# Taking the high and the low part of an operand in one 512-column matmul, in four of seven up products and three of seven down products

## The chip, the cores and the metric

The kernel runs on one core of a Trainium2 chip. The metric is the device time of one execution in microseconds (us), less is better; the number for a kernel is the median of several executions. The profile is of one execution more, recorded by the hardware profiler.

Engines in the text: TensorE (PE in rows; PEld is its weight load), VectorE (DVE), ScalarE (ACT), GpSimd (POOL) and SyncE (SP). SP and POOL issue the transfers here.

## What is computed

One layer of a diffusion backbone over 512 tokens of width 2048 with 256 context tokens: modulated RMSNorm, an input projection, latent attention beside a gated short convolution, an output projection with a residual, and a gated MLP with a width-3 convolution over the tokens. All in float32. The change lies in the MLP:

```python
def conv_ffn(h, w_up, cw, cb, w_down):
    u = dwconv3(h @ w_up, cw, cb)
    a, g = jnp.split(u, 2, axis=-1)
    return (a * jax.nn.silu(g)) @ w_down
...
        hf_l = modulate(rms_norm(x, g_ffn_norm[l]), sh_f, sc_f)
        x = x + gt_f * conv_ffn(hf_l, w_up[l], ffn_conv_w[l], ffn_conv_b[l], w_down[l])
    return rms_norm(x, g_final)
```

`w_up` is 2048 x 11008 and `w_down` 5504 x 2048, so the MLP has 43 tiles of 128 hidden units, each with two up columns (gate and value).

## The kernel before

Activations are kept transposed: 128 features on the partitions, 512 tokens on the free axis. TensorE works on a short float format (float32r), so each float32 factor is split in a high part (a cast, on ScalarE) and a low part (the rest, a subtraction on VectorE). A product of a weight w and an operand x is three matmuls into one PSUM bank: w high by x high, w high by x low, w low by x high. That is `mm3` (L185 to L189, one line for each). Each matmul loads its own 128x128 weights first.

The MLP saves matmuls by Strassen's method in Winograd's form. Two feature tiles by two halves of the tokens (H0 and H1, 256 columns each) are a 2x2 block, and seven products of 256 columns stand in for eight. The operands are sums of such blocks, named "11", "21", "2", "1", "3", "4" and "22"; the products are p1, p2, p6, q5, p7, q4 and q3 in the order of those names.

*Up projection.* The first three of the 43 tiles are done plainly, row by row over 16 operand tiles (`row`, L612). The operand tiles `hf` have the high part in one buffer of 512 columns and the low part in another (`hf_tile`, L931), and so have the sums `TT` of `t_sums` (L1075). Then a loop (L1199) runs over the other 40 tiles f. Each has seven calls of `product` (L1165): `split4` (L995) splits 1024 columns of weights into one of three buffers (high by ScalarE, L998; low by VectorE, L999), and 8 times `mm3` follow, 24 matmuls of 256 columns. Three banks pa, pb and pc take p1, p6, p7 and q4 (pa), p2 (pb), q5 and q3 (pc). VectorE and ScalarE read them out into cg and ca (L1174, L1212, L1224, L1180, L1182); q4 and q3 of a tile are done a turn later, in `finish` (L1177). Then come the convolution and the gate (`acts`, L1010), and every second tile the sums for the down projection (`pair_sums`, L1035), whose results (tp) go to memory over POOL's queue with both parts side by side in 512 columns.

VectorE also adds weights: L1213 (a11 + s1, where s1 is a difference that an accumulating transfer on POOL's queue has made) and L1214.

*Down projection.* Seven hidden tiles are done plainly at 512 columns, the other 36 as 18 pairs: 24 steps (v0 to v23) of seven products over a window of 6 pairs, 18 matmuls each (`seven`, L1319). The operands come back from memory as tiles w with the parts side by side. `into` (L1331) adds a product into its sums in SBUF: L1335 in the first eight steps, L1338, with the gate as a factor, afterwards. Per step VectorE splits seven low parts (L999), makes s3 for the step after (L1290), and after POOL's accumulating transfer into s1 (L1291), which must come behind L1290, the sums L1351 and L1352. The last two steps, v22 and v23, run interleaved, and the final norm follows.

The order on each engine is not that of the code: the framework runs a model of the program over time and puts the instructions of each engine in the order in which they could go there. Each engine then works through its own list strictly, so an instruction that waits holds up all behind it.

Of the kernel before, what the change touches and what calls it, by code (L numbers as in the profile page):

```python
# [10 lines left out]
F32 = mybir.dt.float32  # L11
# [61 lines left out]
def block_kernel(ctx, tc, xt, ctxt, ctxn, c, c_ctx, w_ada, small, w_in, w_inc, w_q, w_kv, w_out,  # L73
# [111 lines left out]
    def mm3(ps, w, x, first, last, on_top=False):  # L185
        with tc.issue_after(behind.pop()) if behind else ExitStack():
            PE.matmul(ps, w[0], x[0], start=first, stop=False, skip_group_check=on_top)  # L187
        PE.matmul(ps, w[0], x[1], start=False, stop=False, skip_group_check=on_top)  # L188
        PE.matmul(ps, w[1], x[0], start=False, stop=last, skip_group_check=on_top)  # L189

# [734 lines left out]

    hf = {}

# [3 lines left out]
    def hf_tile(j, cols=slice(0, T)):  # L931
        if j not in hf:
            hf[j] = tuple(t2([P, T], F32R, f"hf{j}{z}") for z in "hl")
# [6 lines left out]
        hi, lo = (z[:, cols] for z in hf[j])  # L940
        A.copy(out=hi, in_=xr)
        ins = V.tensor_tensor(out=lo, in0=xr, in1=hi.bitcast(F32), op=ALU.subtract)
# [132 lines left out]
    def t_sums(j):  # L1075

        e, o = xres[2 * j], xres[2 * j + 1]
        i, c = j // 2, HS[j % 2]
        if j % 2 == 0:
            for n in (1, 2, 4):  # L1080
                TT[n, i] = tuple(t2([P, T], F32R, f"T{n}{i}{z}") for z in "hl")
# [11 lines left out]
        for n, src in ((1, e[:, H0]), (2, o[:, H1]), (4, o[:, H0])):  # L1093
            put(tuple(z[:, c] for z in TT[n, i]), src)

    def operand(n, j):
        if n in ("11", "3"):
            return half_of(hf[2 * j], n == "3")
        if n in ("21", "22"):
            return half_of(hf[2 * j + 1], n == "22")  # L1100
        return half_of(TT[int(n), j // 2], j % 2)
# [21 lines left out]

    pss = [bank_of(i, f"uf{g}") for g, i in enumerate((2, 3, 4, 5, 1, 0))]
# [3 lines left out]
    for k in range(EARLY):  # L1128
        row(pss, held[k], hf[k], k, H0)
        pump(1)  # L1130
    drain()
    for k in range(EARLY):
        hf_tile(k, H1)
        row(pss, held[k], hf[k], k, H1)
        pump(1)
        if k in (3, 5):
            t_sums(k // 2 - 1)
# [9 lines left out]
    for k in range(EARLY, NK):  # L1147
# [7 lines left out]
        row(pss, w, hf[k], k)  # L1155
# [8 lines left out]

    def product(ps, a, n, nm, first):  # L1165

        w = split4(a, 1024, nm)
        for j in range(8):
            mm3(ps[:, :256], part(w, j), operand(n, j), first and j == 0, j == 7, on_top=not first)
# [7 lines left out]
    def finish(st):  # L1177
        f, a22, s4, u2, u3, pa, pc, cg, ca = st
        product(pa, a22, "4", f"u{f}q4", False)
        A.activation(ca[:, H0], pa[:, :256], AF.Identity, scale=-1.0)  # L1180
        product(pc, s4, "22", f"u{f}q3", False)
        V.tensor_tensor(out=cg[:, H1], in0=pc[:, :256], in1=u2, op=ALU.add)  # L1182
        acts(f, cg, ca)
# [15 lines left out]
    for f in range(G // 2, NF):  # L1199
# [12 lines left out]
        V.tensor_tensor(out=cg[:, H0], in0=pb[:, :256], in1=u1, op=ALU.add)  # L1212
        V.tensor_tensor(out=a11, in0=a11, in1=s1, op=ALU.add)  # L1213
# [10 lines left out]
        V.scalar_tensor_tensor(out=ca[:, H1], in0=pc[:, :256], scalar=-1.0, in1=u3, op0=ALU.mult, op1=ALU.subtract)  # L1224
        if first_acts:
# [50 lines left out]
    def weights_of(st):  # L1276

        z = Step()
        z.st, z.win, z.m = st, window(st), 2 * (st % 8)
        nxt = window(st + 1) if st + 1 < STEPS else z.win  # L1280
# [38 lines left out]
    def seven(z, ps, a, n, nm, first, pump_at=()):  # L1319
# [3 lines left out]
        for j, p in enumerate(z.win):  # L1323
            x = win[n, p]
            mm3(ps[:, :256], part(w, j), (x[:, :256], x[:, 256:]), first and j == 0, j == WIN - 1, on_top=not first)
# [5 lines left out]
    def into(z, i, cols, ps, minus=False):  # L1331

        o = acc2[z.m + i][:, cols]
        if z.st < 8:
            ins = V.tensor_tensor(out=o, in0=o, in1=ps[:, :256], op=ALU.subtract if minus else ALU.add)  # L1335
        else:
            g = ng[:, z.m + i:z.m + i + 1] if minus else mod[:, 80 + z.m + i:81 + z.m + i]
            ins = V.scalar_tensor_tensor(out=o, in0=ps[:, :256], scalar=g, in1=o, op0=ALU.mult, op1=ALU.add)  # L1338
# [255 lines left out]
```

## Time and profile before

| | |
|---|---|
| median of 3 runs | 2148.93 us (2143.85 to 2150.8) |
| the profiled execution | 2158.83 us |
| its span, first to last instruction | 2157.0 us |
| mean granted TensorE clock | 0.994 |
| matmuls | 14458 |
| up projection by seven products | about 886 to 1695 us of the span |
| down projection by seven products | about 1770 to 2150 us |

The rows of a timeline have the start in us, the length in us, the engine, the line of the code, the operation and its tiles (out<-in, buffer numbers left out), the shapes, and in square brackets the idle time before it and what ended that. Matmuls are pipelined, so the next one starts before the recorded end of the last. A row of the stretches has the length, and for each engine its busy time and the number of instructions, then the granted clock of TensorE as a share, the mean busy share of the transfer engines and their GB/s. A row of waits has who waited, for whom, the total in us, the count and the longest.

### The profile page before, as it was taken

How to read it: one execution, taken by the hardware profiler on the slowest of the kernel's cores; microseconds unless marked ns; L12 is line 12 of the kernel's file. 1: busy time of each engine (PE TensorE's matmuls, PEld its weight loads, DVE VectorE, ACT ScalarE, POOL GpSimd, SP SyncE). 2: the span in 40 equal slices, each digit the busy share in tenths (PEclk: the TensorE clock that was granted, in tenths of full speed). 3: DMA queues.
4: the chain of work that ended last, by engine and by line, in shares of the span. 5: the costliest groups of instructions: out<-in, count | busy, mean ns of one | idle time of the engine just before them, and what ended most of it. 6: DMA issues, size and time to landing. Idle time of an engine off the chain costs nothing.

```text
span 2157.0 us, 37744 instructions
## 1 busy us (share of the span) xinstructions
PE 2104.9 (98%) x14458; PEld 1946.7 (90%) x14458; DVE 1769.0 (82%) x2859; ACT 1047.1 (49%) x1710; POOL 188.1 (9%) x270
## 2 busy tenths in 40 slices
PE   7899999999999999999999999999999999999997
PEld 4688788888888888999999999999999889999997
DVE  7998987778886889788888788788888658888877
ACT  5533333555552237555555555555555333333445
POOL 0000000000000000111211111111111000000000
PEclk9999999999999999999999999999999999999998
DMA  9979785334559986577887877877887999877683
GB/s 335 345 275 337 270 279 176 128 126 162 177 199 348 344 278 192 159 217 201 241 232 215 240 229 220 237 231 219 241 229 218 341 335 290 254 220 236 196 247 111
DMA packets 162121, 513.89 MB, mean 238 GB/s; under 512 B 18962, under 2 KB 23314, under 8 KB 156306
## 3 DMA queue, kind: packets, MB, share of 16 engines
q1 hardware_dynamic: 133364, 418.14, 56.5%
q0 software_dynamic: 27488, 92.29, 18.3%
q8 instruction: 113, 1.85, 0.3%
q10 hardware_dynamic: 1088, 1.05, 0.1%
q14 instruction: 68, 0.56, 0.1%
HBM read 464.22 MB, written 46.14 MB: 237 GB/s over the span
## 4 chain that ended last, share of the span: by engine, by line
PE 86%; DVE 6%; DMA 5%; issue 1%; ACT 1%; SPq 0%; DVEq 0%; POOLq 0%; ACTq 0%
PE pp L187 4%; PE pp L189 4%; PE pp L188 4%; PE o L189 1%; PE o L187 1%; PE o L188 1%; DMA ada<-in_w_ada 1%; PE d L187 1%; PE d L189 1%; PE d L188 1%; PE uf L187 1%; PE uf L188 1%; PE of L187 1%; PE of L188 1%; PE of L189 1%
## 5 line engine op out<-in xcount | busy, mean ns | idle before, releaser
L1044 POOL DMA_DIRECT2D t_d<-tp x126 | 71.9, 574 | 468.3 <-DVE tp L1043 465.4
L255 DVE SCALAR_TENSOR_TENSOR ada<-ada,sv 128x1024 f32<-128x1024 f32 x68 | 82.1, 1219 | 12.1 <-DMA ada<-in_w_ada 12.0
L166 ACT CAST w_0h<-rw 128x512 fp32r<-128x512 f32 (+1 forms) x63 | 38.3, 618 | 108.3 <-PE pp L188 63.1
L1121 POOL DMA_DIRECT2D u_s<-in_w_up x80 | 70.2, 878 | 224.4 <-DMA u_s<-in_w_up 131.5
L233 DVE SCALAR_TENSOR_TENSOR ada<-ada,sv 128x1024 f32<-128x1024 f32 x64 | 77.5, 1217 | 4.4 <-DMA ada<-in_w_ada 3.9
L522 DVE SCALAR_TENSOR_TENSOR ada<-ada,svc 128x1024 f32<-128x1024 f32 x64 | 76.0, 1220 | 2.3 <-DMA ada<-in_w_ada 2.3
L785 POOL TENSOR_TENSOR gr<-gr,half 128x8 f32<-128x8 f32 x4 | 10.1, 2524 | 628.7 <-DVE gr L784 536.8
L1042 ACT CAST tp<-a 128x256 fp32r<-128x256 f32 x90 | 34.7, 405 | 60.5 <-DMA t_d<-tp 54.1
L167 DVE TENSOR_TENSOR w_0l<-rw,w_0h 128x512 fp32r<-128x512 f32 (+1 forms) x63 | 42.6, 681 | 22.3 <-ACT w_0h L166 22.3
L255 DVE SCALAR_TENSOR_TENSOR ra<-ra,sv 128x1024 f32<-128x1024 f32 x44 | 52.5, 1217 | 1.1 <-DMA ra<-in_w_ada 1.1
L1213 DVE TENSOR_TENSOR u<-u,u_s 128x1024 f32<-128x1024 f32 x40 | 48.8, 1219 | 0.7 <-DMA u_s<-in_w_up 0.7
L1214 DVE TENSOR_TENSOR u<-u,u 128x1024 f32<-128x1024 f32 x40 | 48.7, 1218 | 0.0
L1043 DVE TENSOR_TENSOR tp<-a,tp 128x256 fp32r<-128x256 f32 x90 | 36.2, 418 | 12.3 <-ACT tp L1042 12.3
L756 ACT CAST pth<-t 128x384 fp32r<-128x384 f32 x64 | 28.6, 485 | 26.4 <-PE t L753 26.4
L1042 ACT CAST tp<-ts 128x256 fp32r<-128x256 f32 x36 | 14.6, 407 | 43.5 <-DMA t_d<-tp 41.1
L533 DVE TENSOR_TENSOR acc<-acc,pp 128x512 f32<-128x512 f32 x50 | 34.0, 680 | 2.1 <-PE pp L189 2.1
L757 DVE TENSOR_TENSOR ptl<-t,pth 128x384 fp32r<-128x384 f32 x64 | 33.2, 549 | 2.7 <-ACT pth L756 2.7
L737 DVE TENSOR_REDUCE mn<-s 128x1 f32<-128x768 f32 x32 | 30.4, 952 | 4.8 <-PE s L726 4.6
L1043 DVE TENSOR_TENSOR tp<-ts,tp 128x256 fp32r<-128x256 f32 x36 | 15.2, 421 | 23.3 <-ACT tp L1042 23.3
L1005 ACT ACTIVATE g<-cg,sm 128x512 f32<-128x512 f32 x40 | 32.5, 813 | 0.5 <-DVE cg L1182 0.5
L1005 ACT ACTIVATE a<-ca,sm 128x512 f32<-128x512 f32 x40 | 32.1, 803 | 0.0
L1013 ACT ACTIVATE g<-g 128x512 f32<-128x512 f32 x43 | 27.2, 632 | 6.4 <-DVE g L1007 6.4
(15967 smaller groups left out, 9398.2 us busy)
## 6 DMA issues: line engine op xcount, KB each, us to landing
ada<-in_w_ada SPq DMA_DIRECT2D x196, 512.0 KB, 6.0
u<-in_w_up SPq DMA_DIRECT2D x120, 512.0 KB, 8.2
w<-t_d SPq DMA_DIRECT2D x161, 256.0 KB, 5.2
u_s<-in_w_up SPq DMA_DIRECT2D x80, 512.0 KB, 4.3
u_s<-in_w_up POOLq DMA_DIRECT2D x80, 512.0 KB, 8.9
t_d<-tp POOLq DMA_DIRECT2D x126, 256.0 KB, 4.9
v<-in_w_dnw SPq DMA_DIRECT2D x72, 384.0 KB, 5.4
ra<-in_w_ada SPq DMA_DIRECT2D x22, 1024.0 KB, 4.9
```

What stands on the lines that cost most here:

```text
L187: PE.matmul(ps, w[0], x[0], start=first, stop=False, skip_group_check=on_top)
L188: PE.matmul(ps, w[0], x[1], start=False, stop=False, skip_group_check=on_top)
L189: PE.matmul(ps, w[1], x[0], start=False, stop=last, skip_group_check=on_top)
L233: V.scalar_tensor_tensor(out=r, in0=r, scalar=1.0, in1=vec[:, i * 1024:(i + 1) * 1024], op0=ALU.mult, op1=ALU.mult, accum_out=col[:, i:i + 1])
L255: keep(V.scalar_tensor_tensor(out=r, in0=r, scalar=1.0, in1=svs[i], op0=ALU.mult, op1=ALU.mult, accum_out=lc[:, t % 4:t % 4 + 1] if i else ...
L522: keep(V.scalar_tensor_tensor(out=raw[q], in0=raw[q], scalar=1.0, in1=svc[:, q * 1024:(q + 1) * 1024], op0=ALU.mult, op1=ALU.mult, accum_o ...
L1005: A.activation(u, src, AF.Identity, bias=s("fb", m), scale=s("fw", 86 + m))
L1042: A.copy(out=z[:, :256], in_=src)
L1043: V.tensor_tensor(out=z[:, 256:], in0=src, in1=z[:, :256].bitcast(F32), op=ALU.subtract)
L1044: G_.dma_start(t_d[p, OPS.index(n)], z.bitcast(F32))
L1121: G_.dma_start(r[-1], src[more], accum_op=ALU.add)
L1213: V.tensor_tensor(out=a11, in0=a11, in1=s1, op=ALU.add)
```

## The change

A new helper `mm2` takes an operand of 512 columns, the high part in the lower 256 and the low part in the upper. One matmul with the high weights runs over all 512 columns, and one with the low weights over the lower 256. The bank then holds w high by x low in its upper half, and VectorE adds that half to the destination in an operation of its own. In the up projection this holds for p2, q5, q4 and q3 (operands "21", "1", "4" and "22") of all 40 tiles; in the down projection for p2, q5 and q3 of the steps v0 to v21. The others keep `mm3`.

For that the operands must lie side by side: the odd tiles of `hf` become two tiles of 512 columns, one for each half of the tokens, and so do all `TT`. The plain rows over odd `hf` tiles run in two halves of 256 columns for that reason (`up_row`).

```diff
+    def mm2(ps, w, x, first, last, on_top=False):
+        n = x.shape[1] // 2
+        with tc.issue_after(behind.pop()) if behind else ExitStack():
+            PE.matmul(ps[:, :2 * n], w[0], x, start=first, stop=False, skip_group_check=on_top)
+        PE.matmul(ps[:, :n], w[1], x[:, :n], start=False, stop=last, skip_group_check=on_top)
...
+    def side_by_side(z, src):
+        n = T // 2
+        A.copy(out=z[:, :n], in_=src)
+        return V.tensor_tensor(out=z[:, n:], in0=src, in1=z[:, :n].bitcast(F32), op=ALU.subtract)
...
+        else:
+            for h in range(2):
+                if cols in (HS[h], slice(0, T)):
+                    hf[j, h] = t2([P, T], F32R, f"hf{j}{h}")
+                    ins = side_by_side(hf[j, h], xres[j][:, HS[h]])
...
+    def up_row(w, k, hs=(0, 1)):
+        if k % 2 == 0:
+            row(pss, w, hf[k], k, slice(hs[0] * 256, hs[-1] * 256 + 256))
+            return
+        for g in range(G):
+            for h in hs:
+                mm3(pss[g][:, HS[h]], w[g], two(hf[k, h]), False, k == NK - 1 and h == 1)
...
+    APART = ("21", "1", "4", "22")
+    def beside(dst, ps, minus=False):
+        V.tensor_tensor(out=dst, in0=dst, in1=ps[:, 256:], op=ALU.subtract if minus else ALU.add)
...
-            mm3(ps[:, :256], part(w, j), operand(n, j), first and j == 0, j == 7, on_top=not first)
+            x = operand(n, j)
+            if n in APART:
+                mm2(ps, part(w, j), x, first and j == 0, j == 7, on_top=not first)
+            else:
+                mm3(ps[:, :256], part(w, j), x if isinstance(x, tuple) else two(x), first and j == 0, j == 7, on_top=not first)
...
         A.activation(ca[:, H0], pa[:, :256], AF.Identity, scale=-1.0)
+        beside(ca[:, H0], pa, True)
         product(pc, s4, "22", f"u{f}q3", False)
         V.tensor_tensor(out=cg[:, H1], in0=pc[:, :256], in1=u2, op=ALU.add)
+        beside(cg[:, H1], pc)
...
         V.tensor_tensor(out=cg[:, H0], in0=pb[:, :256], in1=u1, op=ALU.add)
+        beside(cg[:, H0], pb)
...
         V.scalar_tensor_tensor(out=ca[:, H1], in0=pc[:, :256], scalar=-1.0, in1=u3, op0=ALU.mult, op1=ALU.subtract)
+        beside(ca[:, H1], pc, True)
...
+        z.apart = st < STEPS - 2
...
+            if z.apart and n in APART[:2] + APART[3:]:
+                mm2(ps, part(w, j), win[n, p], first and j == 0, j == WIN - 1, on_top=not first)
+            else:
+                mm3(ps[:, :256], part(w, j), two(win[n, p]), first and j == 0, j == WIN - 1, on_top=not first)
...
+        for x in (ps[:, :256], ps[:, 256:])[:2 if z.apart and ps is not z.pa else 1]:
+            if z.st < 8:
+                ins = V.tensor_tensor(out=o, in0=o, in1=x, op=ALU.subtract if minus else ALU.add)
+            else:
+                g = ng[:, z.m + i:z.m + i + 1] if minus else mod[:, 80 + z.m + i:81 + z.m + i]
+                ins = V.scalar_tensor_tensor(out=o, in0=x, scalar=g, in1=o, op0=ALU.mult, op1=ALU.add)
```

Three places show what moves. The lines of the changed kernel have numbers of their own: 1024 there is 999 before, 1257 and 1258 are 1213 and 1214, 1337 is 1290, 1388 is 1338, 1401 and 1402 are 1351 and 1352. The new addition in the up projection is 1200.

TensorE at the start of product p2 of up tile 20 (bank u20b; hf are operand tiles, u20p2h and u20p2l the two parts of the weights), before:

```order
L187 MATMUL u20b<-hf1h,u20p2h 128x256
L188 MATMUL u20b<-hf1l,u20p2h 128x256
L189 MATMUL u20b<-hf1h,u20p2l 128x256
L187 MATMUL u20b<-hf3h,u20p2h 128x256
L188 MATMUL u20b<-hf3l,u20p2h 128x256
L189 MATMUL u20b<-hf3h,u20p2l 128x256
```

and after the change:

```order
L196 MATMUL u20b<-hf_7575,u20p2h 128x512
L197 MATMUL u20b<-hf_7575,u20p2l 128x256
L196 MATMUL u20b<-hf_7676,u20p2h 128x512
L197 MATMUL u20b<-hf_7676,u20p2l 128x256
L196 MATMUL u20b<-hf_7691,u20p2h 128x512
L197 MATMUL u20b<-hf_7691,u20p2l 128x256
```

Three instructions per operand tile have become two, with the same number of columns in all.

VectorE from the low part of p1 of up tile 21 on, around that of p2 (u21p2l; the sum of u_11 and u_s is the one that waits for the accumulating transfer; a, g, ts and tp belong to the convolution and the sums for the down projection), before:

```order
L1213 TENSOR_TENSOR u_11_12589<-u_11_12589,u_s_12593 128x1024
L1015 TENSOR_TENSOR a_12748<-a_12748,g_12743 128x512
L999 TENSOR_TENSOR u21p2l<-u_12_12591,u21p2h 128x1024
L1048 TENSOR_TENSOR ts_13016<-a_12748 128x256
L999 TENSOR_TENSOR u20q4l<-u_22_12349,u20q4h 128x1024
L1214 TENSOR_TENSOR u_12_12591<-u_12_12591,u_11_12589 128x1024
```

and after:

```order
L1086 SCALAR_TENSOR_TENSOR a_12125<-ts_12158,a_12125 128x256
L1040 TENSOR_TENSOR a_12365<-a_12365,g_12360 128x512
L1024 TENSOR_TENSOR u21p2l<-u_12_12229,u21p2h 128x1024
L1257 TENSOR_TENSOR u_11_12227<-u_11_12227,u_s_12231 128x1024
L1068 TENSOR_TENSOR tp_12354<-a_12125,tp_12354 128x256
L1073 TENSOR_TENSOR ts_12605<-a_12365 128x256
L1024 TENSOR_TENSOR u20q4l<-u_22_12015,u20q4h 128x1024
```

The sum of u_11 has gone from ahead of u21p2l to behind it.

VectorE in the down projection, from the low part of p1 of step 13 on (c are the sums; v13b and v11c the banks of p2 and of q5 and q3; v13s and v14s the weights that the accumulating transfers change), before:

```order
L999 TENSOR_TENSOR v13p1l<-v_21392,v13p1h 128x768
L1351 TENSOR_TENSOR v_21392<-v_21392,v13s_21393 128x768
L1338 SCALAR_TENSOR_TENSOR c_18809<-v11c,mod,c_18809 128x256
L999 TENSOR_TENSOR v13p2l<-v_21394,v13p2h 128x768
L1338 SCALAR_TENSOR_TENSOR c_19122<-v12a,gn,c_19122 128x256
L1352 TENSOR_TENSOR v_21394<-v_21394,v_21392 128x768
L999 TENSOR_TENSOR v12q4l<-v_21199,v12q4h 128x768
L1338 SCALAR_TENSOR_TENSOR c_19124<-v13a,mod,c_19124 128x256
L999 TENSOR_TENSOR v13p6l<-v_21392,v13p6h 128x768
L1290 TENSOR_TENSOR v14s_21592<-v_21589,v14s_21590 128x768
L1338 SCALAR_TENSOR_TENSOR c_19124<-v13b,mod,c_19124 128x256
```

and after:

```order
L1388 SCALAR_TENSOR_TENSOR c_17789<-v11c,mod,c_17789 128x256
L1401 TENSOR_TENSOR v_20197<-v_20197,v13s_20198 128x768
L1388 SCALAR_TENSOR_TENSOR c_17789<-v11c,mod,c_17789 128x256
L1024 TENSOR_TENSOR v13p2l<-v_20199,v13p2h 128x768
L1388 SCALAR_TENSOR_TENSOR c_18102<-v12a,gn,c_18102 128x256
L1024 TENSOR_TENSOR v12q4l<-v_20019,v12q4h 128x768
L1402 TENSOR_TENSOR v_20199<-v_20199,v_20197 128x768
L1388 SCALAR_TENSOR_TENSOR c_18104<-v13a,mod,c_18104 128x256
L1024 TENSOR_TENSOR v13p6l<-v_20197,v13p6h 128x768
L1388 SCALAR_TENSOR_TENSOR c_18104<-v13b,mod,c_18104 128x256
L1337 TENSOR_TENSOR v14s_20382<-v_20379,v14s_20380 128x768
L1388 SCALAR_TENSOR_TENSOR c_18104<-v13b,mod,c_18104 128x256
```

The additions out of v11c and v13b come twice, one of each pair on either side of a sum; the first one out of v13b is now ahead of the sum of v14s; and the low part of q4 is ahead of the sum of v_20199 and no longer behind it.

36 lines of the change are left out of this document (15 added, 21 removed).

## The prediction

> **What bounds the kernel now.** I read the page first, then the busy time by stretch, then the timelines of TensorE and VectorE inside the two stages that the diff touches, then who waits for whom.
>
> The head of the page gives the span and each engine's share:
>
> ```profile
> span 2157.0 us, 37744 instructions
> PE 2104.9 (98%) x14458; PEld 1946.7 (90%) x14458; DVE 1769.0 (82%) x2859; ACT 1047.1 (49%) x1710; POOL 188.1 (9%) x270
> ```
>
> TensorE is busy 98% of the span and VectorE 82%. A busy share says little about pipelined matmuls, so I went on to stretches. The rows are the up projection, the first down steps, the middle ones and the tail:
>
> ```profile
> core 0: us, PE busy (x) PEld busy (x) DVE busy (x) ACT busy (x) POOL busy (x), PEclk, DMA share, GB/s
> 895.00:1695.00 800.00, 798.99 (x6647) 798.23 (x6646) 656.33 (x867) 454.99 (x681) 140.16 (x209) 1.00 0.80 229
> 1775.00:1850.00 75.00, 74.34 (x620) 73.59 (x619) 65.15 (x110) 28.80 (x35) 3.74 (x5) 1.00 0.92 292
> 1850.00:2060.00 210.00, 210.00 (x1753) 210.00 (x1752) 174.76 (x248) 83.37 (x101) 11.58 (x14) 1.00 0.76 225
> 2060.00:2157.00 97.00, 80.69 (x646) 78.48 (x644) 71.37 (x110) 47.99 (x85) 3.41 (x4) 0.94 0.56 169
> ```
>
> In the up projection TensorE has no gap (798.99 of 800 us) at a granted clock of 1.00; VectorE is at 82%. The middle down steps are the same (210 of 210 us, VectorE 83%). What one matmul costs is the distance between starts, not its recorded length. Here are the ends of one product of the up projection (tile 19, product p2), 24 matmuls of 256 columns, and the first of the next one:
>
> ```profile
> 1204.14 0.28 PE L187 MATMUL u19b<-hf1h,u19p2h 128*128 128x256 f32 x1
> ...
> 1207.02 0.28 PE L187 MATMUL u18a<-T40h,u18q4h 128*128 128x256 f32 x1
> ```
>
> 24 starts in 2.88 us: 120.0 ns each. The output projection has the same work 512 columns wide, 44 matmuls from the first row to the second:
>
> ```profile
> 739.70 0.39 PE L187 MATMUL o<-mx13h,o9w1536h 128*128 128x512 f32 x1
> ...
> 749.92 0.39 PE L189 MATMUL o<-mx11h,o10w1024l 128*128 128x512 f32 x1
> ```
>
> 10.22 us / 44 = 232.3 ns. So 512 columns in one matmul cost 7.7 ns less than in two (240.0). That is all that the change can win on TensorE, many times over.
>
> **The change, part by part.**
>
> *The matmuls.* In the up projection 40 tiles x 4 products x 8 triples = 1280 triples of 256 columns become a pair of 512 and 256; in the down projection 22 steps x 3 products x 6 = 396. A triple costs 3 x 120.0 = 360.0 ns. For the pair, alternating widths are hardly in the trace; the nearest rows are the attention scores, five matmuls of 512 columns and then five of 256:
>
> ```profile
> 505.25 0.40 PE L722 MATMUL s<-kl11h,q11h 128*128 128x512 f32 x1
> ...
> 506.41 0.28 PE L722 MATMUL s<-kcx,q11h 128*128 128x256 f32 x1
> ...
> 507.00 0.69 PE L371 MATMUL qr<-xq,kc 128*128 128x512 f32 x1
> ```
>
> From 505.25 to 507.00 five of each take 1.75 us: 350 ns per pair, with no penalty where the width changes. The two paces above give 232.3 + 120.0 = 352.3. I take 351: 9 ns per triple (bounds 7.7 and 10). Up: 1280 x 9 = 11.5 us (9.9 to 12.8). Down: 396 x 9 = 3.6 us (3.0 to 4.0). All of it lies on TensorE, which has no gap there, so it is on the path as long as nobody else makes TensorE wait.
>
> The Trainium skill, "TensorE: Matmul & The Clock Gate", Back-to-back issue gap, gives N / 2.4 + 2.5 ns for a warm matmul: an estimate from that page is 109.2 ns at 256 columns and 215.8 at 512, so a triple would save only 2.6 ns and the whole change 4.4 us. The trace disagrees with both numbers (120.0 and 232.3 at a granted clock of 1.00).
>
> *The first product by rows.* Odd operand tiles now lie as two half tiles, so from tile 6 on the rows of 7, 9, 11, 13 and 15 run as 36 matmuls of 256 columns and not 18 of 512: 90 pairs x 7.7 ns = 0.7 us more. Splitting such a tile in two halves adds an operation each on ScalarE and VectorE, beside a row of 18 x 232.3 ns = 4.2 us on TensorE; nothing without that cover, 0.4 us a tile at the most.
>
> *VectorE's additions, up.* Each product that takes both parts leaves its second half in the upper 256 columns, and VectorE must add it: four more operations per tile. The nearest row reads a bank and adds, in the finishing of a tile:
>
> ```profile
> 1234.88 0.42 DVE L1182 TENSOR_TENSOR cg<-u19c,u 128x256 f32<-128x256 f32 x1
> 1235.22 0.41 DVE L1061 SCALAR_TENSOR_TENSOR a<-ts,a 128x256 f32<-128x256 f32 x1
> ```
>
> The next one starts 0.34 us later: 4 x 0.34 = 1.4 us per tile, 0.42 each where one must wait for the other's result. A tile takes 7 x 24 x 120 ns = 20.16 us, of which VectorE is idle 18%, 3.6 us. It has 2.2 us left, less the 0.3 us by which the tile gets shorter. So VectorE stays under TensorE on the mean; what counts is the queue in front of the low parts of the weights. The tightest one in the up projection is p2 of the odd tiles:
>
> ```profile
> 1242.84 1.22 DVE L999 TENSOR_TENSOR u21p2l<-u,u21p2h 128x1024 fp32r<-128x1024 f32 x1
> ```
>
> ```profile
> 1244.70 0.28 PE L189 MATMUL u21b<-hf1h,u21p2l 128*128 128x256 f32 x1
> ```
>
> The low part is done at 1244.06 and read at 1244.70: 0.64 us to spare, the least in steady state. In the new order the big sum of this tile goes behind u21p2l and not in front of it, which gives back 1.1 us of the 1.4. I take 1.0 us of new waits for the whole stage; bounds are zero and 20 odd tiles x 0.4 us = 8 us.
>
> *VectorE's additions, down.* Three more per step, in the middle steps of the form of L1338. Here VectorE also feeds itself: its sum for the next step (L1290) must be done before the accumulating transfer that POOL issues, and the step after next to it begins with L1351, which waits for that transfer. The rows are one turn of that loop, the low part q4 in it, and the transfer:
>
> ```profile
> 1977.00 0.96 DVE L1351 TENSOR_TENSOR v<-v,v14s 128x768 f32<-128x768 f32 x1 [1.02 <-DMA v14s<-in_w_dnw]
> 1980.40 0.95 DVE L999 TENSOR_TENSOR v13q4l<-v,v13q4h 128x768 fp32r<-128x768 f32 x1
> 1981.27 0.48 DVE L1338 SCALAR_TENSOR_TENSOR c<-v14a,mod,c 128x256 f32<-128x256 f32 x1
> 1981.66 0.95 DVE L999 TENSOR_TENSOR v14p6l<-v,v14p6h 128x768 fp32r<-128x768 f32 x1
> 1982.65 0.96 DVE L1290 TENSOR_TENSOR v15s<-v,v15s 128x768 f32<-128x768 f32 x1
> ```
>
> ```profile
> L1291 POOL DMA_DIRECT2D v15s<-in_w_dnw x1: 850/850/850, 1984.1 to 1984.1; - x1
> ...
> DMA to landing us min/median/max: 5.1/6.8/7.8
> ```
>
> From L1351 to POOL's issue it is 7.1 us, the transfer takes 6.8 (5.1 to 7.8): 13.9 us of the step's 126 x 120 ns = 15.12. An addition costs 0.39 us (1981.27 to 1981.66). In the new order one of the three stands between L1351's successor and L1290's, since the one after p2 now comes ahead of the sum: 14.3 us of the new step's 14.96 (15.12 less 18 x 9 ns), 15.3 where the transfer takes 7.8. The low part of q4 goes ahead of the second big sum, 0.87 us earlier, so it loses nothing. Some steps wait already; of TensorE's waits in the down projection:
>
> ```profile
> PE v19a L189 <- DVE v19q4l L999: 0.9, 1, 0.9
> PE v20a L189 <- DVE v20q4l L999: 0.9, 1, 0.9
> PE v21a L189 <- DVE v21q4l L999: 0.9, 1, 0.9
> ```
>
> Such steps, some seven at both ends of the stage, turn with the loop and not with TensorE, and each becomes longer by the addition in it: 7 x 0.39 = 2.7 us. The bounds are zero and all three additions uncovered in every step, 22 x 3 x 0.42 = 28 us; I take the loop's 2.7, since the middle steps have room.
>
> *The sum.* -11.5 + 0.7 + 1.0 - 3.6 + 2.7 = -10.7 us. The profiled execution took 2158.83 us (span 2157.0, 1.8 around it) and would take 2148.1. The runs' median is 2148.93, 9.9 us below the profiled one; the same difference gives 2138.
>
> **The rivals.**
>
> *A: the remaining 256-column matmuls get faster as well.* The pace of 120.0 ns holds through the whole up projection, but in the first down steps it is less:
>
> ```profile
> 1775.51 0.28 PE L188 MATMUL v0a<-w,v0p6h 128*128 128x256 f32 x1
> ...
> 1780.49 0.28 PE L188 MATMUL v0a<-w,v0p7h 128*128 128x256 f32 x1
> ```
>
> 42 starts in 4.98 us are 118.6 ns. So 120.0 is not what 256 columns need; a stream of mixed widths could leave that beat. Then 3 x 24 x 1.4 ns x 40 = 4.0 us come on top, the pair costs 350, and with few waits it is -12.8 - 4.0 - 4.0 + 0.7 = -20 us: 2129. Against it: the up projection comes out of a row product 512 columns wide and is at 120.0 at once.
>
> *B: the beat holds for the wide ones too.* If starts between 256-column matmuls keep to multiples of 120 ns, the pair takes 240 + 120 = 360 and nothing is won; the same result on the clock if waits for VectorE eat the 11 us. For it: the exact 120.0. Against it: the scores change from 512 to 256 without loss. TensorE then takes as long as now, so few waits are new; with the 0.7 of the rows it is 2150, within the bound of no change. The page's rule above stands close to it: less the same cost its 4.4 us would give an estimate of 2145.
>
> *C: VectorE becomes the bound, and it is slower.* The loop of L1351, L1290 and the transfer has 0.6 us left with a transfer of 6.8. It decides from the point where the transfer takes over 7.4 us on the mean. From step 18 to 19 the loop already took 16.1 us, with an addition of squares in it:
>
> ```profile
> 2036.54 0.96 DVE L1351 TENSOR_TENSOR v<-v,v18s 128x768 f32<-128x768 f32 x1
> ...
> 2052.64 0.96 DVE L1351 TENSOR_TENSOR v<-v,v19s 128x768 f32<-128x768 f32 x1 [1.06 <-DMA v19s<-in_w_dnw]
> ```
>
> At 16.1 us a step, 16 steps from 6 to 21 lose 16 x 1.0 = 16 us; with 8 us of waits at the odd tiles of the up projection and 11.5 won, it is +13: 2162. Against it: the transfer's median of 6.8, and a new order that was made with the additions in it.
>
> **How the numbers follow.** A measurement of this kernel tells about 0.3% (6.4 us) from no change. Forecast 0.57, A 0.15, B 0.18, C 0.10. The time is the forecast's, 2138. Low is A with a little more, 2127; high is B, 2150; beyond it lie C and the worse half of B. The forecast crosses 6.4 us where waits reach 5.5 us more than I took: 3 in 57 of it count as no change. Faster 0.54 + 0.15 = 0.69, same 0.03 + 0.18 = 0.21, slower 0.10.
>
> **What would show it.** Right: one product of the four in the up projection takes 8 x 351 = 2.81 us and not 2.88, a tile 19.88 us with 7 products, no wait of TensorE over 0.5 us in it, VectorE at 90%. Wrong in size: the pair at 360 (B), or p1, p6 and p7 under 2.86 us (A). Wrong in kind: TensorE waiting for low parts in the steps 6 to 18, or L1351's successor waiting for its transfer over 2 us in each (C).

## The result: slower by 3.2%, 2218.17 us

The changed kernel takes 2218.17 us in the median of 4 runs (2215.94 to 2222.97), the kernel before 2149.86 in the median of 4 (2143.85 to 2155.02). The ratio is 1.0322, with a 95% interval of 1.029 to 1.0354. The forecast was 2138, and none of the rivals came to this time.

The head of the page of the changed kernel, and the busy time of its up projection and of its middle down steps (columns as in the prediction: the stretch and its length, PE, PEld, DVE, ACT, POOL, granted clock, DMA share, GB/s):

```profile
span 2216.3 us, 34748 instructions
...
PE 2112.3 (95%) x12872; PEld 1878.4 (85%) x12872; DVE 1845.8 (83%) x3090; ACT 1051.9 (47%) x1715; POOL 187.7 (8%) x270
```

```profile
895.00:1695.00 800.00, 755.86 (x5027) 699.93 (x5025) 668.90 (x962) 431.22 (x638) 132.49 (x197) 0.97 0.75 211
...
1920.00:2110.00 190.00, 186.81 (x1347) 176.14 (x1348) 169.16 (x262) 73.52 (x90) 11.08 (x13) 1.00 0.74 219
```

TensorE, which had no gap in the up projection before (798.99 of 800 us), now stands still for 44 of 800 us, and the granted clock is 0.97 and no longer 1.00. VectorE is hardly busier in this stretch than before (84% against 82%), although it has four operations more per tile, because fewer tiles fall into these 800 us.

Where the 59.3 us between the two spans arise is read from the first matmul of each stage:

| stage (TensorE) | before | after | difference |
|---|---|---|---|
| all ahead of the first product by rows | 815.16 | 810.42 | -4.7 |
| first product by rows | 69.3 | 71.0 | +1.7 |
| up projection, seven products a tile | 801.8 | 856.7 | +54.9 |
| down projection, plain steps | 83.9 | 87.9 | +4.0 |
| down projection, seven products a step, to the last matmul | 376.8 | 380.2 | +3.4 |

The first line is no effect of the change: in the runs below this part ends anywhere from 810.0 to 817.3 us. Nor is the fourth: of its 4.0 us, 2.1 are one wait for a load in this execution, and a run below with the same order takes 84.1 us there.

**The matmuls did what was forecast.** In TensorE's timeline, product q5 of tile 18 with the wide matmuls, and p6 with the narrow ones:

```profile
1200.20 0.28 PE L187 MATMUL u18a<-T,u18p6h 128*128 128x256 f32 x1
...
1202.34 0.28 PE L187 MATMUL u18a<-T,u18p6h 128*128 128x256 f32 x1
...
1202.69 0.40 PE L196 MATMUL u18c<-T,u18q5h 128*128 128x512 f32 x1
...
1205.15 0.40 PE L196 MATMUL u18c<-T,u18q5h 128*128 128x512 f32 x1
```

From the third row to the fourth are seven pairs: 2.46 us, 351 ns each. From the first to the second are six triples: 2.14 us, 357 ns each, so the narrow ones run at 118.9 ns and not at 120.0 (rival A's pace). A tile without a wait takes 19.77 us; it took 20.16.

**The loss is at p1 of the odd tiles.** TensorE's waits in the up projection, longest first (who waits, on whom; us in total, times, longest):

```profile
PE u13a L187 <- ACT u13p1h L1023: 4.2, 1, 4.2
PE u25a L187 <- ACT u25p1h L1023: 3.8, 1, 3.8
...
PE u37a L187 <- ACT u37p1h L1023: 2.2, 1, 2.2
```

There are 15 of them, from tile 13 to 41, every second tile, 43.6 us in all. Nothing of the kind was there before. They wait for ScalarE's high part of the weights, not for VectorE's low part. ScalarE's timeline at tile 19, after and then before (L1067 and L1042 are the cast of a pair sum into its tile tp; in brackets the idle time ahead of an instruction and who ended it):

```profile
1202.10 0.81 ACT L1030 ACTIVATE a<-ca,sm 128x512 f32<-128x512 f32 x1
1206.92 0.40 ACT L1067 CAST tp<-a 128x256 fp32r<-128x256 f32 x1 [4.02 <-DMA t_d<-tp]
1207.23 1.04 ACT L1023 CAST u19p1h<-u 128x1024 fp32r<-128x1024 f32 x1
1208.18 0.37 ACT L1215 COPY u<-u18a 128x256 f32<-128x256 f32 x1
```

```profile
1195.58 1.05 ACT L998 CAST u19p1h<-u 128x1024 fp32r<-128x1024 f32 x1 [0.41 <-PE u18a L188]
1196.54 0.36 ACT L1174 COPY u<-u18a 128x256 f32<-128x256 f32 x1
1199.68 0.41 ACT L1042 CAST tp<-a 128x256 fp32r<-128x256 f32 x1 [2.78 <-DMA t_d<-tp]
```

Before, the cast into tp waited 2.78 us with the p1 weights already cast. After, it waits 4.02 us, and the p1 weights of tile 19 and the copy of bank u18a stand behind it. It waits for its buffer: only two t2 buffers rotate among the pair sums, and a buffer is free when its store has landed. The store it waits for, in POOL's timeline, and its way to landing (KB, us) in the list of transfers:

```profile
1196.01 0.86 POOL L1144 DMA_DIRECT2D u_s<-in_w_up  x1 [1.01 <-DMA u_s<-in_w_up]
1196.58 0.86 POOL L1069 DMA_DIRECT2D t_d<-tp  x1
```

```profile
t_d<-tp POOLq DMA_DIRECT2D x1, 256.0 KB, 10.3
```

Issued at 1196.58, it lands 10.3 us later, at 1206.9: that is when the cast starts. The median store lands after 5.2 us; this one was issued right behind an accumulating load of 512 KB. TensorE at the same place:

```profile
1205.38 0.28 PE L197 MATMUL u18c<-T,u18q5l 128*128 128x256 f32 x1
1208.33 0.39 PE L187 MATMUL u19a<-hf0h,u19p1h 128*128 128x256 f32 x1 [2.66 <-ACT u19p1h L1023]
...
1208.67 0.31 PE L187 MATMUL u18a<-hf0h,u18p7h 128*128 128x256 f32 x1
...
1209.12 0.41 PE L187 MATMUL u18a<-hf2h,u18p7h 128*128 128x256 f32 x1
...
1212.11 0.40 PE L189 MATMUL u18a<-hf10h,u18p7l 128*128 128x256 f32 x1
```

Two matmuls of p1 stand ahead of p7 of the tile before (in the kernel before as well), so TensorE stops as soon as q5 is through. When it goes on, 14 starts take 2.99 us, 213.6 ns each instead of 119: half clock, about 1.5 us more (the granted clock from 1208.90 to 1212.30 is 0.51, behind it 1.00). Counted in starts, the 14 long gaps up to tile 39 come to 42.3 us and the half clock behind them to 19.2 us: 61.5 us.

### The profile page after: what moved, and what is told of

It is laid out like the page before. It is cut to its first block, busy times and chain, and to the rows that moved or that the text cites. A ratio compares the mean times of both kernels' runs of the same rounds, so it can differ in the third digit from the quotient of the medians.

```text
span 2216.3 us, 34748 instructions
## 1 busy us (share of the span) xinstructions
PE 2112.3 (95%) x12872; PEld 1878.4 (85%) x12872; DVE 1845.8 (83%) x3090; ACT 1051.9 (47%) x1715; POOL 187.7 (8%) x270
## 4 chain that ended last, share of the span: by engine, by line
PE 66%; DMA 16%; DVE 11%; issue 3%; ACT 3%; POOL 0%; DVEq 0%; SPq 0%; POOLq 0%; ACTq 0%
DMA t_d<-tp 7%; DMA u_s<-in_w_up 4%; PE pp L187 4%; PE pp L189 4%; PE pp L188 4%; PE o L188 1%; PE o L187 1%; PE o L189 1%; DMA ada<-in_w_ada 1%; PE d L187 1%; PE uf L187 1%; PE uf L188 1%; PE uf L189 1%; PE d L188 1%; PE of L188 1%
## 5 line engine op out<-in xcount | busy, mean ns | idle before, releaser
L1069 POOL DMA_DIRECT2D t_d<-tp x126 | 78.9, 626 | 525.0 <-DVE tp L1068 513.7
L1144 POOL DMA_DIRECT2D u_s<-in_w_up x80 | 69.8, 872 | 233.9 <-DMA u_s<-in_w_up 147.3
L1067 ACT CAST tp<-a 128x256 fp32r<-128x256 f32 x90 | 34.8, 406 | 100.0 <-DMA t_d<-tp 92.6
L793 POOL TENSOR_TENSOR gr<-gr,half 128x8 f32<-128x8 f32 x4 | 10.1, 2522 | 627.7 <-DVE gr L792 535.6
L1294 DVE SCALAR_TENSOR_TENSOR aq<-aq,svq 128x512 f32<-128x512 f32 x32 | 21.2, 687 | 10.8 <-DMA aq<-in_w_ada 10.0
L748 ACT ACTIVATE p<-s,mn 128x768 f32<-128x768 f32 x32 | 29.3, 915 | 1.6 <-DVE mn L745 1.3
```

Of the source, the lines that this page charges most:

```text
L1069: G_.dma_start(t_d[p, OPS.index(n)], z.bitcast(F32))
L1144: G_.dma_start(r[-1], src[more], accum_op=ALU.add)
```

## The experiments

Theory 1: the order on ScalarE. A cast into tp that waits for a store now stands ahead of what TensorE needs next; matmuls and VectorE's load are innocent. Rival 2: VectorE's added work makes the weights late. Rival 3: the stores are too slow, whatever stands behind them. A fourth reading is the order alone, without a wait for a store. The table gives all runs. Each ratio, with its 95% interval, is to the kernel before as it was measured beside that run (2149.9 to 2153.0 us). The stages are read as above, from TensorE's timeline of one profiled execution each; the down stage differs by several us between kernels whose down code is the same (376.8, 372.4 and 370.1 in the three kernels without wide matmuls).

| kernel | median us | ratio (interval) | up, seven products | down, seven products |
|---|---|---|---|---|
| before | 2149.86 | 1 | 801.8 | 376.8 |
| after | 2218.17 | 1.0322 (1.029, 1.0354) | 856.7 | 380.2 |
| casts behind | 2154.61 | 1.0009 (0.9995, 1.0023) | 792.7 | 382.0 |
| before, tp ahead | 2166.65 | 1.0078 (1.0056, 1.0101) | 819.0 | 372.4 |
| put at every second product | 2218.98 | 1.031 (1.0284, 1.0336) | 857.5 | 381.4 |
| no additions, tp ahead | 2176.51 | 1.0119 (1.0094, 1.0144) | 820.0 | 372.5 |
| no additions | 2146.46 | 0.9973 (0.9958, 0.9987) | 786.6 | 376.4 |
| stores of a resident tile | 2170.54 | 1.009 (1.0064, 1.0115) | 810.0 | 373.5 |
| first matmuls of p1 behind p7 | 2248.02 | 1.0456 (1.0437, 1.0475) | 882.9 | 378.7 |
| four buffers | 2265.59 | 1.0527 (1.0501, 1.0553) | 868.2 | 405.2 |
| early steps narrow | 2145.94 | 0.9966 (0.9951, 0.9982) | 794.1 | 373.3 |
| puts at four products | 2139.89 | 0.9938 (0.9918, 0.9957) | 788.4 | 370.5 |
| the same, late steps narrow | 2140.86 | 0.9943 (0.9922, 0.9963) | 787.3 | 370.6 |
| before, puts at four products | 2153.44 | 1.0003 (0.999, 1.0015) | 802.9 | 370.1 |

**Casts behind the weights: the order undone, all else kept.**

```
     w = split4(a, 1024, nm)
+    with tc.issue_after(last_hi[0]):
+        pump(1)
     for j in range(8):
...
-    pump(1)
```

> The changed kernel with every wide matmul and every addition kept; each put of a pair sum is issued only behind the weight cast of a product, so on ScalarE no cast into tp stands ahead of the p1 cast of an odd tile any more. Theory 1 (a cast into tp that waits for the store of the put two before stands ahead of the p1 weights, and TensorE waits and then runs at half clock): the 15 waits of 2.2 to 4.2 us and the half clock behind them go, a pair of up tiles takes 39.6 us instead of 44.1, the up stage by seven products some 795 us instead of 857, the kernel 2150 us (2140 to 2165; what the rows stage, the plain down stage and the down loop lost stays). Rival 2 (the work added to VectorE makes the weights late): nothing of that load is gone, 2218 us as before (2210 to 2225). Rival 3 (the stores themselves are too slow, whatever stands behind them): the waits move to another product's cast, 2190 to 2220 us.

2154.61 us: 63.6 us of the loss are gone, with every wide matmul and every addition still there. The edit moves the casts into tp at all products, not only at p1. ScalarE at tile 19:

```profile
1187.13 1.04 ACT L1023 CAST u19p1h<-u 128x1024 fp32r<-128x1024 f32 x1
1188.08 0.36 ACT L1216 COPY u<-u18a 128x256 f32<-128x256 f32 x1
1191.50 0.41 ACT L1067 CAST tp<-a 128x256 fp32r<-128x256 f32 x1 [3.06 <-DMA t_d<-tp]
```

The cast into tp still waits 3.06 us for a store, and it costs nothing, since p1 and the copy stand ahead of it. This speaks against rival 2 and rival 3 at once: the stores are slower still (7.7 us to landing in the median, 5.2 in the changed kernel), and VectorE's load is all there, 692.67 of 765 us (91%) in the stretch from 895 to 1660 of the up projection, with TensorE at 762.07:

```profile
895.00:1660.00 765.00, 762.07 (x5220) 706.41 (x5219) 692.67 (x1002) 441.89 (x663) 138.02 (x206) 1.00 0.80 228
```

**The kernel before, with the cast into tp ahead of p1.**

```
-    last_hi[:] = [A.copy(out=hi[:, :n], in_=src).ins]
+    with tc.issue_after(last_tp.pop()) if last_tp and nm[-2:] == "p1" and int(nm[1:-2]) % 2 else ExitStack():
+        last_hi[:] = [A.copy(out=hi[:, :n], in_=src).ins]
...
-            A.copy(out=z[:, :256], in_=src)
+            last_tp[:] = [A.copy(out=z[:, :256], in_=src).ins]
```

> The kernel before, no wide matmul, no addition, the old tiles; one edit: the weight cast of p1 of the odd tiles is issued behind the cast into tp that belongs to the product ahead of it (with it the copy of p6's result comes ahead too). One cast in 14 changes its place. Theory 1: TensorE waits at p1 of the odd tiles as in the changed kernel, 16 times 1.5 to 4.5 us and half clock behind it: 25 to 70 us slower, 2175 to 2220 us. Rival 2 (VectorE's load): nothing is added to VectorE, 2150 us within 0.3 per cent. Rival 3 (stores): between, since the casts wait 2.9 us in the mean now: 2150 to 2200 us.

2166.65 us, below the range of theory 1, yet 17 us slower with nothing added to VectorE. The place of one cast is enough for a loss; but TensorE's longest waits are far shorter than in the changed kernel:

```profile
PE u13b L187 <- ACT u13p2h L999: 1.0, 1, 1.0
...
PE u27a L187 <- ACT u27p1h L999: 0.9, 1, 0.9
```

In this kernel the copy of p6's result stood ahead of the cast into tp, as the expectation says, and in the odd tiles the first matmuls of p1 had come to stand behind p7. So neither was held up where TensorE asked for it at once.

**A put at every second product.**

```
-    pump(1)
+    pumps[0] ^= 1
+    pump(pumps[0])
```

> The changed kernel, but a pair sum is put out at every second product instead of at seven products in a row and then none for seven: the same puts, stores, buffers and additions, and the cast into tp stays ahead of the p1 cast of the odd tiles. A store has twice the time before its buffer is wanted again. Theory 1: a cast in that place costs only when its buffer isn't free; the store has landed, no wait at p1, 2150 us (2140 to 2165). A theory of the order alone, without the stores: 2218 us as before. Rival 2 (VectorE's load as a mean): as much work in the mean, only spread; 2200 to 2218 us.

2218.98 us, as the changed kernel. This run decides nothing on the stores, since the edit hardly moved the casts: on ScalarE they stand 15 times ahead of p1 and 31 times ahead of p6, as in the changed kernel, and their waits for stores come to 118.9 us in the whole run. What it shows is that the same order gives the same time.

**No additions, with the cast into tp tied ahead, and without the tie.** The edit of the first is `return` in place of the addition's line, and the tie of the run above; the second has the `return` alone.

> The changed kernel without the four additions in the up projection: its output lacks the products of the weights' high parts with the operands' low parts for four of the seven products there. That alone would also undo the order on ScalarE, so the p1 cast of the odd tiles is tied behind the cast into tp, as it stands in the changed kernel. Theory 1: the waits at p1 of the odd tiles stay without any of VectorE's added work, 2185 to 2225 us. Rival 2 (VectorE's load): 40 x 4 x 0.34 us = 54 us less on VectorE, and with it the loss: 2125 to 2150 us.

> The changed kernel without the four additions in the up projection (its output lacks the products of the weights' high parts with the operands' low parts for four of the seven products there), with the order that ScalarE gets then: no cast into tp ahead of p1. Beside the run in which that order was tied back (2176.5 us) it prices the order without VectorE's added work, beside the run with all additions and the order mended (2154.6 us) it prices the additions themselves. Theory 1: the additions cost little by themselves, 2145 to 2155 us, the order some 25 us. Rival 2 (VectorE's load costs by itself, whatever the order): 25 us or more below the run with the order mended, 2130 us or less.

2176.51 and 2146.46 us. Without the additions the casts into tp leave p1 by themselves, so it was the additions that moved them. The loss comes through that order and not through VectorE's time: with all additions and the casts behind the kernel takes only 8 us more than without additions. Tying the cast ahead costs 30 us without any added work on VectorE. That is less than theory 1 had set (2185 or more), and for the same reason as in the kernel before: there, too, the copy stood ahead of the cast.

**Stores of a resident tile: the order kept, the wait gone.**

```
-    G_.dma_start(t_d[p, OPS.index(n)], z.bitcast(F32))
+    G_.dma_start(t_d[p, OPS.index(n)], hf[1, 0].bitcast(F32))
```

> The changed kernel, but each of the 126 stores of pair sums sends a resident operand tile instead of the tile just filled, so that its buffer is free without the store: the same number, size and place of stores and transfers, the same casts and additions, and the cast into tp still ahead of the p1 cast in 15 tiles; its output lacks the pair sums. Theory 1 (the cast waits for a store that lands some 10 us after its issue, since it is queued behind an accumulating load of 512 KB): without that wait the cast in that place costs 0.4 us on ScalarE, the up stage by seven products takes some 795 us, the kernel 2150 us (2140 to 2165). A theory of the order alone: 2200 to 2220 us.

2170.54 us, 5 above the range. The stores, which no longer depend on a cast, did not keep their place: all 126 were issued between 815 and 962 us. Tiles 4 to 6 took 25.2, 30.0 and 27.4 us (22.7, 17.0 and 19.8 in the changed kernel). From tile 7 on no tile is longer than 19.84 us, with the cast into tp ahead of p1:

```profile
1210.34 0.41 ACT L1067 CAST tp<-a 128x256 fp32r<-128x256 f32 x1
...
1212.07 1.04 ACT L1023 CAST u19p1h<-u 128x1024 fp32r<-128x1024 f32 x1
```

So the order alone costs nothing; it needs the wait for the store. The flaw of this run is that from tile 7 on the traffic of the stores is missing too. The run with the casts behind has all that traffic and no loss, so traffic without the order doesn't cost either. Together the two runs say that it takes both.

**The first matmuls of p1 behind p7.** Behind the last matmul of p7, by the same means that holds a matmul elsewhere:

```
+    if j == 0 and nm[-2:] == "p1" and last_p7:
+        behind.append(last_p7.pop())
...
+        if nm[-2:] == "p7":
+            last_p7[:] = [ins]
```

> The changed kernel with one edit on TensorE: the first two matmuls of p1 of a tile, which stand ahead of the 24 of p7 of the tile before it (in the kernel before as well), are issued behind them. The cast into tp stays ahead of the p1 cast of the odd tiles, 15 times, with its wait for the store. The two runs in which that cast was tied ahead lost only 17 to 26 us where the changed kernel lost 64, and in both TensorE's order had these two matmuls behind p7 in the odd tiles. Theory 1, completed by this (the wait shows whole because two matmuls ask for the p1 weights one product, 2.85 us, before the rest of p1 does): the waits of 2.2 to 4.2 us fall to 0 to 1.4, nearly all below the length after which the half clock came, and the kernel takes 2165 us (2155 to 2180). Rival (the smaller loss there came from the missing additions and the other places of the casts): the waits stay, 2205 us or more.

2248.02 us: slower still, and the completed theory fell in this point. ScalarE and then TensorE at tile 18 of this run:

```profile
1215.27 0.40 ACT L1067 CAST tp<-ts 128x256 fp32r<-128x256 f32 x1 [5.67 <-DMA t_d<-tp]
...
1217.30 1.04 ACT L1023 CAST u19p1h<-u 128x1024 fp32r<-128x1024 f32 x1
1218.25 0.36 ACT L1220 COPY u<-u18a 128x256 f32<-128x256 f32 x1
```

```profile
1218.66 0.58 PE L187 MATMUL u18a<-hf0h,u18p7h 128*128 128x256 f32 x1 [4.33 <-ACT u L1220]
```

p7 adds on top of p6 in bank u18a, so it must wait until the copy has taken p6's result out, and that copy stands behind the p1 cast and so behind the cast into tp. In the changed kernel the same copy ends at 1208.55 and p7 starts at 1208.67 (above). Two things that TensorE needs stand in that queue, and freeing it of one doesn't help; that here the wait is even longer (5.67 us) comes with a second cast into tp that moved behind p7's weights. That the copy ahead would have made the difference in the two tied runs is read from these rows; a kernel with the copy alone moved wasn't tried.

**Four buffers for the pair sums.**

```
-    z = t2([P, T], F32R, f"tp{p}{n}")
+    turn2[0] ^= 1
+    z = t2([P, T], F32R, f"tp{p}{n}") if turn2[0] or p == PAIRS - 1 else tpp.tile([P, T], F32R, tag="tp", bufs=2, name=f"tp{p}{n}")
...
-        return rw.tile([P, 1024], F32, tag="raw", bufs=9, name=nm)
+        return rw.tile([P, 1024], F32, tag="raw", bufs=8, name=nm)
```

> The changed kernel with four buffers instead of two for the pair sums on their way out, paid with one of the nine buffers of the weight loads; ScalarE gets another order by itself, with no cast into tp ahead of p1. Theory 1: no waits at p1, up stage some 795 us, 2150 us (2145 to 2157). Rival (eight buffers for loads make the weights late): 2165 us or more.

2265.59 us, as the rival said. Casts wait less for stores (66.7 us in the stage instead of 117.1), but the ninth load buffer was worth more: VectorE's sum now waits for its accumulating load, in 36 of 40 tiles, against 2.8 us in all in the changed kernel:

```profile
DVE u L1261 <- DMA u_s<-in_w_up: 117.7, 36, 5.6
```

On more buffers alone it says nothing.

**The down loop.** With the order mended the up projection was 9.1 us shorter than before and the kernel still no faster. Its seven-product down steps 3 to 8 took up to 17.2 us (15.1 to 15.9 before). VectorE and TensorE in step 6 of that run:

```profile
1845.40 0.96 DVE L1402 TENSOR_TENSOR v<-v,v6s 128x768 f32<-128x768 f32 x1 [2.84 <-DMA v6s<-in_w_dnw]
...
1846.61 0.95 DVE L1024 TENSOR_TENSOR v6p2l<-v,v6p2h 128x768 fp32r<-128x768 f32 x1
```

```profile
1847.62 0.38 PE L197 MATMUL v6b<-w,v6p2l 128*128 128x256 f32 x1 [0.78 <-DVE v6p2l L1024]
```

This is the loop of the prediction's rival C, in the early steps only: VectorE, which has the residual's sums there as well, waits 2.84 us for the accumulating transfer, and TensorE for the low part behind it. So in that run, with its casts behind, the early steps were made narrow:

```
-        z.apart = st < STEPS - 2
+        z.apart = 9 <= st < STEPS - 2
```

> The run with the order mended (2154.6 us; its pair of stages by down products 5 us longer than in the kernel before), and in the down loop the steps 0 to 8 take the three narrow matmuls again; only steps 9 to 21 keep the wide one. Theory: in the early steps VectorE has the residual's sums too and no time left, so the added sums push back the addition for which the accumulating load of the next step waits, and that load's landing holds the low parts (2.84 us in step 6): without them in steps 0 to 8 the down loop falls by 6 to 9 us, 2147 us (2142 to 2150). Rival: the early steps wait for the loads by themselves: no change, 2153 to 2156 us.

2145.94 us; the down loop fell by 8.7 us to 373.3, the size that the theory had. That the added sums by themselves make the early steps slow is not shown, though. The tied run without the additions in the up projection keeps all wide matmuls of the down loop and has the same order on VectorE from step 1 on, and it took 372.5 us; in the run with stores of a resident tile, wide as well, steps 1 to 19 took 14.9 to 15.0 us each. What differs is the accumulating transfer: those for steps 6 to 8 landed after 7.1 to 7.5 us in the run with the casts behind, and after 5.6 to 6.5 in these two. The sums cost where the transfer is slow, and what makes it slow stays open.

**The puts at four products.** The remaining waits of up to 1.0 us stood at p2 of the odd tiles, again behind a cast into tp.

```
+        if nm[-2:] in ("p6", "q5", "q4", "q3"):
+            with tc.issue_after(last_hi[0]):
+                pump(1)
         for j in range(8):
...
-        pump(1)
```

> The run with the order mended and steps 0 to 8 narrow (2145.9 us), and a put is now issued only behind the weight casts of p6, q5, q4 and q3, so that no cast into tp stands ahead of p1 or p2, whose weights come latest; all additions and wide matmuls of the up projection stay. Its up stage by seven products took 794.1 us, the run without additions 786.5. Theory 1: what is left between these is casts into tp ahead of the p2 weights of odd tiles (waits of 1.0 us there), so the stage falls to 787 to 789 us and the kernel to 2140 us (2136 to 2143). Rival 2 (the additions cost that themselves, through VectorE): 794 us, 2146 us.

> The kernel before with that same place for the puts, and nothing else: no wide matmul, no addition. Theory: its casts into tp cost TensorE nothing where they stood, so nothing changes, 2152 us (within 0.3 per cent of the kernel before); then the gain of the mended kernel is the wide matmuls' alone. Rival (the place of the puts is a gain of its own): 2140 to 2146 us.

> The run with the puts at four products, and steps 20 and 21 of the down loop narrow too, where TensorE waited 2.1 us for the low part of p2 of step 21. Theory (the added sums hold VectorE there as in the early steps): 2 to 3 us less than the run beside it. Rival (the loads of the last steps come late by themselves; the kernel before had 16.2 and 16.4 us there too): the same within 1 us.

2139.89 us, 2153.44 us and 2140.86 us. The first is a version faster than both kernels, ratio 0.9938 (0.9918 to 0.9957); its page, and the busy times from 895 to 1660 of this kernel and of the kernel before with the same puts:

```profile
span 2134.6 us, 35076 instructions
...
PE 2084.5 (98%) x13034; PEld 1863.3 (87%) x13034; DVE 1832.7 (86%) x3063; ACT 1049.6 (49%) x1715; POOL 188.0 (9%) x270
```

```profile
895.00:1660.00 765.00, 764.35 (x5247) 709.29 (x5246) 692.87 (x1005) 445.68 (x666) 137.89 (x205) 1.00 0.82 229
```

```profile
895.00:1660.00 765.00, 764.42 (x6369) 763.80 (x6368) 633.11 (x834) 437.87 (x654) 136.07 (x202) 1.00 0.79 225
```

TensorE has next to no gaps in either; the one needs 788.4 us for the stage, the other 802.9. So the 14.5 us lie in the matmuls' pace and not in waits, and the place of the puts is worth nothing without the wide matmuls. But not all of it is the width's. Narrow matmuls run at two paces. These are seven triples of tile 23 in the kernel before with tp ahead, which has no wide matmul:

```profile
1287.06 0.28 PE L187 MATMUL u23b<-hf3h,u23p2h 128*128 128x256 f32 x1
...
1289.55 0.28 PE L187 MATMUL u22a<-T40h,u22q4h 128*128 128x256 f32 x1
```

21 starts in 2.49 us are 118.6 ns, and tiles without a wait take 19.94 us in that kernel, not 20.16. The kernel before with the puts moved has one such tile too, tile 21. Beside 19.94 the wide matmuls' 19.77 us are a gain of 0.17 us a tile, 6.8 us over 40; the rest of the 14.5 is the faster pace. All kernels with wide matmuls had it in the up projection; in these two it set in without them, behind a wait of TensorE. Making the last steps narrow changed nothing that can be told.

## Why the prediction was wrong, point by point

- **The step that failed** is the one on VectorE's additions in the up projection: "what counts is the queue in front of the low parts of the weights", with 1.0 us of new waits (bounds 0 to 8). The additions were weighed on the engine that does them. That they also shift the order on ScalarE was not looked at, and ScalarE casts the high parts and copies the banks out. The new order put a cast into tp, which waits for a store, ahead of both: +64 us between the changed kernel and the run with the casts behind. A tied cast alone brought 17 to 30 us of it; the rest is put down to the copy of p6's result, which stood ahead in those two runs and which no run moved by itself. No rival held this; C had the sign, with another mechanism. The hint stood among the waits of before: in the up projection ScalarE waited longest for these very stores (us in total, times, longest), and all of it was hidden by the place of the casts:

```profile
ACT tp L1042 <- DMA t_d<-tp: 95.2, 62, 2.9
```

- **VectorE itself** was judged rightly. Where nothing else disturbs, it is 91% busy in the up projection (forecast: 90%), and the stage with all additions is 1.8 us longer than without (788.4 against 786.6, with the puts in other places); 1.0 was forecast. Its low parts did not hold TensorE in the up projection.
- **The matmuls.** The pair: 351 ns, as taken. In the up projection a tile without a wait takes 0.39 us less, 15.6 us over 40, and not 11.5, since the narrow ones went from 120.0 to 118.9 as well: rival A's pace. Rival B, the pair at 360, is out. But the 360.0 for a triple was the slower of two paces. At 118.7 a triple costs 356, so the pair saves 5 ns and not 9. The prediction had seen that pace in the first down steps and took it for what a mixed stream might bring; narrow matmuls alone have it too.
- **In the down projection** the -3.6 us were nearly nothing. In the kernel before with moved puts, whose down projection is that of the kernel before, a narrow step takes 14.95 us, 118.7 ns a matmul; with wide matmuls it takes 14.91. The 15.12 of the profile of before is the same code at 120.0. The term was worked out from one execution's pace.
- **The down loop's +2.7 us** named the loop in which TensorE did wait, but had size and place wrong: up to 8.7 us, in the early steps, and only in the kernels in which the transfer was slow (above). Both ends of the stage were counted in; narrow late steps brought nothing.
- **The rows of odd tiles** were forecast at +0.7 us; the runs with the order mended took 69.8 us there against 69.3.
- **The sum** of -10.7 us is close to the -12.5 us of the version with ScalarE's order and the early steps set right. That is luck in part. Against the kernel before with the puts moved, its up projection is 14.5 us shorter, over half of it by the pace (forecast: 10.5 with the waits), and its down projection 0.4 longer (forecast: 0.9 shorter). As it stood, the change cost 68.

## What to carry to other kernels

Work added to one engine can move the instructions of another, when the order is worked out for all of them together: compare the order of every engine that feeds the one at the bound, and look there for an instruction that waits for something slow (a store, a load, a buffer) and has come to stand ahead of something urgent. A long wait that costs nothing in a profile is cover, not absence of risk: note what stands ahead of it, and what would if it moved. If a change loses, undo its side effect on the order before judging the change: here the same matmuls and additions gave 1.032 in one order and 1.001 in another, and 0.994 once the puts had their place and the early down steps were narrow.

## What the runs showed of the hardware

- **Half clock after short gaps.** Over the profiles of all 14 kernels, from 870 us on, take the gaps between starts that stand alone (what goes beyond the usual distance, no other gap over 0.3 us close by). Of 63 gaps of 0.9 to 1.8 us none was followed by a row of starts at half pace (about 213 ns for 256 columns); of 64 gaps of 1.8 to 3.2 us 34 were, and of 25 longer ones all. Gaps of 1.23, 1.34 and 1.45 us in the run without additions and with tp tied ahead were followed by it too, but each had a second gap of 1.12 us 1.5 us behind it. The Trainium skill, "TensorE: Matmul & The Clock Gate", The HAM clock gate, has half rate after an idle window of about 3.4 us, and full rate after about 3.4 us of work. The second agrees (3.4 us of half clock from 1208.94 to 1212.33); for the first, shorter gaps were enough here in about half of the cases from 1.8 us on.
- **A 256-column matmul has two paces**, 120.0 and 118.7 to 118.9 ns, at the same granted clock of 1.00, and the same down code ran at either in two kernels. The pace changed where a start came late: from 120.0 to 118.6 at 1035 us in the kernel before with tp ahead (0.6 us late), and in the kernel before with the puts moved to the faster one at 1233 us (0.3 us late) and back at 1277 (less than 0.1). Which way it goes, and why, stays open.
- **A store lands late when an accumulating load is under way on the same queue.** In the changed kernel, 46 stores of 256 KB were issued with nothing of POOL's queue outstanding and landed after 3.8 us in the median (2.3 to 8.0); 63 were issued with an accumulating load of 512 KB outstanding and took 10.1 us (3.7 to 12.2).
